# A hybrid decoder block: sums of input blocks taken from PSUM, and two plain projections made a pair of Strassen products

## The chip, the cores and the metric

The kernel runs on one core of a Trainium2 chip, in one launch. The metric is device time in microseconds, the median of several runs. Five engines work side by side and meet through semaphores: PE (TensorE, matrix products), DVE (VectorE), ACT (ScalarE), POOL (GpSimd) and SP (SyncE, which here only starts transfers). Each engine takes its own instructions in order.

## The reference

Sixteen learned tokens are put ahead of 1024 tokens of width 1024. One layer runs over the 1040 positions, and the output is the normalised rows of the 1024 real tokens.

```python
u = rms_norm(h, norm_w)
proj = u @ w_in                       # 1024 x 9232
(a_q, a_k, a_v, a_z, g_q, g_k, g_v, g_z, g_lr, gate_a, gate_b) = jnp.split(proj, ...)
...                                   # differential attention: a_q, a_k, a_v, a_z -> y_a
gk = (g_lr @ gla_gate_w2 + gla_gate_b).astype(jnp.float32)
lg = jax.nn.log_sigmoid(gk) / GLA_GATE_NORMALIZER
o_b = rms_norm(gla(qb, kb, vb, lg), gla_norm_w)   # gated linear attention
...                                   # y_b
merged = jax.nn.sigmoid(gate_a) * y_a + jax.nn.sigmoid(gate_b) * y_b
return h + merged @ w_out
```

The change concerns `u @ w_in` alone: how the columns g_q (four heads of 128) and g_k (four heads of 128) are made, and what is prepared for the other columns.

## The kernel before, in words

**Precision.** Every product is of float32 accuracy. Both operands are split into a high part in float32r (PE's one-pass format) and a low part, the rest; a product is three matmuls: high by high, high by low, low by high. ACT writes a high part (a copy), DVE or POOL the low part (a subtraction).

**Stage 1 (0 to about 111 us), lines 636 to 940.** Nine tiles of x (eight of 128 tokens and one of the 16 learned ones, the meta tokens) are loaded; ACT squares each with a running sum, DVE and POOL make the root, DVE scales the tile (`x_tile`). PE turns it around, chunk by chunk of 128 of the 1024 features, into PSUM (`u_chunk(g, kc)`: g is the half of the tokens, kc the chunk). ACT takes u_hi out of the bank, DVE u_lo. Beside it run the *plain* projections (`Jobs.cols`, lines 406 to 408): the four g_k tiles of 128 columns over all 1040 tokens in four pieces (`KP4`), and the g_q tiles 16 and 19 over the 1024 real tokens in two pieces of 512. Each piece is 24 matmuls into one of two banks, copied out by ACT (line 765, `stg`) and stored. The low-rank part of the gate (`lr_piece`) is of the same kind, with 48 columns and a chain of small steps on ACT and DVE behind it.

**The block sums, lines 829 to 863.** With u cut in halves by feature (i) and by token (j) into b_ij, Winograd's form of Strassen's product needs t1 = b12 - b11, t2 = b22 - t1, t3 = b12 - b22 and t4 = b21 - t2, split in two parts each. Before, each sum is made of the parts in SBUF, for each of four chunks k: three adds for t1 and t3 (high minus high, plus low, minus low), two for t2 and t4. t1, t2, t4 are DVE's, t3 is POOL's. A tile `bs` holds a sum till ACT has written its high part and DVE or POOL its low part.

**Stage 2, Strassen (from about 111 us).** `Strassen.run` takes two tiles of 128 columns at a time (a *pair*): seven products of half size, 12 matmuls of 512 columns each, 84 in all, where the plain way needs 96 (line 543). POOL makes the sums of weights (line 491), ACT and DVE split them (lines 225 and 226), DVE adds the results (line 557), ACT copies the first product out once in each pair (line 618). Before there are 21 such pairs, the g_q tiles 17 and 18 the first, and two of another form with the tokens on the partitions.

**Later stages.** Gated linear attention, differential attention, the two branch products and the output, from about 600 us on. The change does not touch them.

**What sets the order.** In stage 1 each operation is handed to `Schedule` with an engine, a rough duration, what it depends on, the ring of buffers that it takes and a priority; a simulation of the engines then writes the order of PE, DVE, ACT and POOL. So a new operation moves others on its engine. SP's order comes from the framework. Rings that matter: `X`, six PSUM banks for the turned chunks; `Y`, two banks for projections; `xt`, five tiles for x, and for the block sums later.

Of the kernel before, what the change touches and what calls it, by code (L numbers as in the profile page):

```python
# [10 lines left out]
F32 = mybir.dt.float32  # L11
# [35 lines left out]
GQ = False  # L47
NX = 5
XS = (0, 1, 2, 3, -1, 4, 5, 6, 7)
SCU = 0.6  # L50
T4E = "DVE"
# [18 lines left out]
class Schedule:  # L70
    """Puts operations in order: a simulation of the engines with rough durations, in which each takes
    the ready operation of the lowest priority number. A ring is a tile with so many buffers: an
    operation takes the next one, which is free when all operations that use it are done."""
# [18 lines left out]
    def run(self):  # L92
# [9 lines left out]
        def at(o):  # L102
            """when its data and its buffer are there"""
# [46 lines left out]
def tile_hybrid_block(  # L150
# [52 lines left out]
    for i in range(1, 5):  # L203
        tsum[i] = tuple(tpool.tile([P, KC // 2, 512], F32R, name=f"t{i}{p}") for p in "hl")
# [23 lines left out]
    # ---- weights and projections  # L228
# [15 lines left out]
    # what becomes of the projections  # L244
# [43 lines left out]
    def av_ev(g):  # L288
        """values of four heads, split, to DRAM"""
# [22 lines left out]
    def gv_ev(g):  # L312
        """values of two heads of the other branch, to DRAM"""
# [23 lines left out]
    class Jobs:  # L337
        """Projections as operations that fill the tensor engine; their sums go to the banks of ring Y."""
# [77 lines left out]
        def rows(self, src, evac, pre=None):  # L416
# [19 lines left out]
            # the first and last two in turns, for the weights of this job and of the next to come in time  # L436
# [15 lines left out]
    # ---- Winograd's form of Strassen's product: seven products of half the size for eight.  # L452
    # A: weights, halves by output column (two tiles of 128) and by row; B: halves by row and by token
    class Strassen:
# [72 lines left out]
        def run(self, over):  # L527
# [10 lines left out]
            def prod(ps, b, start):  # L538
                wh, wl = weights()
                bh, bl = self.b[b]  # L540
                for k in range(KC // 2):
                    for i, (w, x) in enumerate(((wh, bh), (wh, bl), (wl, bh))):
# [3 lines left out]
                            x[:, k],  # L546
# [13 lines left out]
            def prod_rows(ps, b, start, meta=()):  # L560
                # the first product in a bank clears it for both of its tiles of tokens
                bh, bl = self.b[b]
                for s in range(2):
                    wh, wl = weights()
                    for k, ti in ((2 * s + j, ti) for ti in range(4) for j in range(2)):
                        c, r = slice(P * ti, P * (ti + 1)), slice(256 * (ti % 2), 256 * (ti % 2 + 1))
                        for i, (x, w) in enumerate(((bh, wh), (bh, wl), (bl, wh))):
                            mm(  # L568
                                ps[ti // 2][:, r],
                                x[:, k, c],  # L570
# [62 lines left out]
    # ---- u^T = rms_norm([meta; x])^T, split into two float32r parts, and the first projections  # L633
# [3 lines left out]
    KP4 = ((0, 264), (264, 264), (528, 256), (784, 256))  # L637
    with ExitStack() as es:
# [49 lines left out]

        def u_chunk(g, kc):
# [13 lines left out]
            for p in range(2):  # L703
# [6 lines left out]
                    use=(own,), prio=10 * g + kc)  # L710
            U[g, kc] = lo

        def u_meta():
# [18 lines left out]
            def diff():  # L732
                """of the halves"""
# [24 lines left out]
        # g_q and g_k of the heads, by DRAM; the low-rank part of the gate  # L758
# [69 lines left out]
        # the sums of the blocks of u: t1 = b12 - b11, t2 = b22 - t1, t3 = b12 - b22, t4 = b21 - t2  # L828
        def sums(k):
            v = {}  # L830
            b = {
                (i, j): [t[:, k + 4 * i, NM + 512 * j : NM + 512 * j + 512].bitcast(F32) for t in (u_hi, u_lo)]
                for i in range(2)
                for j in range(2)
            }
            d = tuple(U[g, k + 4 * i] for g in range(2) for i in range(2))
            own = {}

            def term(name, eng, steps, deps, use):
                ring = "xt"  # L840
                f = tt if eng == "DVE" else nc.gpsimd.tensor_tensor
                us = 0.6 if eng == "DVE" else 1.2
                prev = d + deps

                for i, (x0, x1, o) in enumerate(steps):
                    def run(i=i, x0=x0, x1=x1, o=o):
                        if i == 0:
                            v[name] = s1.tile([P, 512], F32, name="bs", tag="xt", bufs=NX)
                        g = lambda y: v[y] if isinstance(y, str) else y
                        f(v[name], g(x0), g(x1), o)  # L850

                    prev = (op(eng, us, run, prev, take="" if i else ring, use=use, prio=30 + k),)
                    own[name] = own.get(name) or (ring, prev[0])
                hi, lo = (tsum[int(name[1])][p][:, k] for p in range(2))
                a = op("ACT", 0.48, lambda: nc.scalar.copy(hi, v[name]), prev, use=(own[name],), prio=30 + k)
                op(eng, us, lambda: f(lo, v[name], hi.bitcast(F32), ALU.subtract), (a,), use=(own[name],), prio=30 + k)
                return prev

            add, sub = ALU.add, ALU.subtract
            p1_ = term("t1", "DVE", [(b[0, 1][0], b[0, 0][0], sub), ("t1", b[0, 1][1], add), ("t1", b[0, 0][1], sub)], (), ())  # L860
# [1611 lines left out]
```

## Time and profile before

| what | value |
|---|---|
| median of 3 runs | 1407.32 us (1405.42 to 1411.9) |
| profiled execution, span from first to last instruction | 1406.7 us, 0.6 below the median (no other time of it is listed) |
| PE busy | 1339.3 us, 95% |
| DVE busy | 923.8 us, 66% |
| ACT busy | 734.2 us, 52% |
| POOL busy | 646.7 us, 46% |
| mean granted TensorE clock | 0.992 of full speed |
| chain that ended last | PE 66%, DVE 17%, issue 5%, DMA 5%, POOL 3%, ACT 3% |

A busy share is an average over stages with different limits, so a change in one stage has to be read from that stage. The chain of waits is followed back from the last instruction: at each step to what released it. Matmuls overlap in the records, so a matmul's cost is the distance between starts, or a window's time over its count, and not the duration of one.

### The profile page before, as it was taken

The numbers are of one execution on the slowest core, as the hardware profiler recorded it, in microseconds if no ns is written. First come the engines' busy times: TensorE is split into PE (matmuls) and PEld (weight loads), VectorE is DVE, ScalarE is ACT, GpSimd is POOL, SyncE is SP. The second block draws the span as 40 slices with busy tenths as digits, with TensorE's granted clock in tenths as the row PEclk, the third lists the DMA queues.
The fourth block names the chain that finished last, engine by engine and source line by source line (L and its number), as shares of the span: only waits on it lengthen the run. The fifth ranks groups of instructions, "written<-read, shape, count | busy, mean of one in ns | idle before, by whom it ended". The sixth has DMA issues, their size and how long they took to land.

```text
span 1406.7 us, 22441 instructions
## 1 busy us (share of the span) xinstructions
PE 1339.3 (95%) x7748; PEld 1159.6 (82%) x7748; DVE 923.8 (66%) x1613; ACT 734.2 (52%) x1596; POOL 646.7 (46%) x743
## 2 busy tenths in 40 slices
PE   7889999999999999988999989999999999999998
PEld 6877889889888888887888888888888888887786
DVE  5953563554656444469897887478777778647775
ACT  7333332563566656554545444468677776622343
POOL 3521332352355232226575565246676665535434
PEclk9999999999999999999999999999999999999999
DMA  6212674323422333285532456668865664578332
GB/s 219 86 57 90 195 254 137 105 105 109 141 98 105 112 113 113 97 272 160 184 103 98 139 185 204 212 204 287 300 190 183 207 218 144 204 274 284 136 116 87
DMA packets 126337, 229.50 MB, mean 163 GB/s; under 512 B 13568, under 2 KB 51648, under 8 KB 126224
## 3 DMA queue, kind: packets, MB, share of 16 engines
q1 hardware_dynamic: 125936, 227.03, 48.8%
q8 instruction: 61, 1.00, 0.3%
q0 software_dynamic: 288, 1.05, 0.3%
q14 instruction: 52, 0.43, 0.1%
HBM read 143.81 MB, written 84.21 MB: 162 GB/s over the span
## 4 chain that ended last, share of the span: by engine, by line
PE 66%; DVE 17%; issue 5%; DMA 5%; POOL 3%; ACT 3%; SPq 1%; POOLq 0%; DVEq 0%; ACTq 0%
PE ps_st L543 27%; PE ps_st L568 6%; DVE xl L1352 2%; PE ps_t L2268 2%; DVE bs L850 2%; PE ps_s L1645 2%; PE ps_s L1646 2%; PE ps_y L1928 2%; PE ps_proj L406 2%; PE ps_proj L407 1%; PE ps_proj L408 1%; PE ps_t L1759 1%; PE ps_l L1359 1%; PE ps_s L2268 1%; PE ps_y L2268 1%
## 5 line engine op out<-in xcount | busy, mean ns | idle before, releaser
L491 POOL TENSOR_TENSOR s<-w_raw 128x512 f32<-128x512 f32 x46 | 66.6, 1465 | 163.1 <-DMA w_raw<-in_w_col_dram 121.2
L1345 POOL TENSOR_TENSOR xl<-lg 128x128 f32<-128x128 f32 x224 | 108.3, 510 | 59.5 <-PE ps_l L1359 21.7
L406 PE MATMUL ps_proj<-u_hi,w_hi 128*128 128x346 f32 (+4 forms) x352 | 117.9, 335 | 8.8 <-ACT stg L765 5.2
L226 DVE TENSOR_TENSOR wl<-s,wh 128x512 fp32r<-128x512 f32 x92 | 73.2, 795 | 77.1 <-ACT wh L225 77.1
L407 PE MATMUL ps_proj<-u_lo,w_hi 128*128 128x346 f32 (+4 forms) x352 | 111.0, 315 | 0.0
L408 PE MATMUL ps_proj<-u_hi,w_lo 128*128 128x346 f32 (+4 forms) x352 | 110.9, 315 | 0.0
L225 ACT CAST wh<-s 128x512 fp32r<-128x512 f32 x92 | 56.8, 618 | 99.1 <-PE ps_st L543 52.6
L1674 DVE TENSOR_REDUCE nm<-ps_s 128x1 f32<-128x272 f32 (+7 forms) x128 | 96.5, 764 | 17.5 <-PE ps_s L1648 16.7
L1686 ACT ACTIVATE p<-ps_s,nm 128x272 f32<-128x272 f32 (+7 forms) x128 | 96.5, 755 | 19.4 <-DVE nm L1674 13.5
L543 PE MATMUL ps_st<-u_lo,wh 128*128 128x512 f32 x252 | 100.2, 398 | 0.0
L543 PE MATMUL ps_st<-u_hi,wh 128*128 128x512 f32 x252 | 99.4, 395 | 0.8 <-issue 0.8
L543 PE MATMUL ps_st<-u_hi,wl 128*128 128x512 f32 x252 | 99.1, 393 | 0.0
L225 ACT CAST wh<-w_raw 128x512 fp32r<-128x512 f32 x67 | 41.3, 617 | 91.1 <-PE ps_st L543 83.6
L226 DVE TENSOR_TENSOR wl<-w_raw,wh 128x512 fp32r<-128x512 f32 x67 | 58.6, 875 | 42.1 <-ACT wh L225 42.1
L491 POOL TENSOR_TENSOR s<-w_raw,s 128x512 f32<-128x512 f32 x21 | 27.1, 1292 | 120.2 <-DVE wl L226 120.2
L1698 POOL TENSOR_SCALAR p<-p,r,nlam 128x144 f32<-128x144 f32 (+3 forms) x64 | 56.4, 881 | 56.3 <-DVE r L1694 43.9
L406 PEld LDWEIGHTS ps_proj<-u_hi,w_hi 128*128 128x128 f32 x352 | 67.0, 190 | 12.7 <-ACT stg L765 6.0
L1645 PE MATMUL ps_s<-kk,q 128*128 128x264 f32 (+7 forms) x208 | 74.0, 360 | 2.1 <-ACT p L1686 1.9
L1703 DVE SCALAR_TENSOR_TENSOR p<-p,r,p 128x144 f32<-128x144 f32 (+3 forms) x64 | 67.8, 1060 | 11.1 <-POOL p L1698 10.9
L1646 PE MATMUL ps_s<-kk,q 128*128 128x264 f32 (+7 forms) x208 | 68.6, 334 | 0.0
L407 PEld LDWEIGHTS ps_proj<-u_lo,w_hi 128*128 128x128 f32 x352 | 66.9, 190 | 1.6
L408 PEld LDWEIGHTS ps_proj<-u_hi,w_lo 128*128 128x128 f32 x352 | 66.7, 190 | 1.4
(441 smaller groups left out, 4611.9 us busy)
## 6 DMA issues: line engine op xcount, KB each, us to landing
w_raw<-in_w_col_dram SPq DMA_DIRECT2D x54, 512.0 KB, 3.6
q<-d_q SPq DMA_DIRECT2D x32, 512.0 KB, 5.3
kk<-d_k SPq DMA_DIRECT2D x16, 520.0 KB, 6.1
d_g<-sg SPq DMA_DIRECT2D x32, 256.0 KB, 2.0
va<-d_v SPq DMA_DIRECT2D x16, 512.0 KB, 5.1
d_q<-qhi SPq DMA_DIRECT2D x24, 256.0 KB, 3.2
d_q<-qlo SPq DMA_DIRECT2D x24, 256.0 KB, 3.5
w_raw<-in_w_row_dram SPq DMA_DIRECT2D x12, 512.0 KB, 3.7
```

The lines of the kernel that those rows point to most:

```text
L225: nc.scalar.copy(hi, raw)
L226: (eng or nc.vector).tensor_tensor(lo, raw, hi.bitcast(F32), ALU.subtract)
L406: mm(b["ps"], wh, rh, start=kc == 0, stop=False)
L407: mm(b["ps"], wh, rl, start=False, stop=False)
L408: mm(b["ps"], wl, rh, start=False, stop=kc == KC - 1)
L491: nc.gpsimd.tensor_tensor(r, x, y, op)
L543: mm(ps, w[:, k], x[:, k], start=start and k == 0 and i == 0, stop=k == KC // 2 - 1 and i == 2, skip_group_check=not start,)
L1345: nc.gpsimd.tensor_tensor(dst, x if e else ref, ref if e else x, ALU.subtract)
L1645: mm(pp, qh, kk[:, c0 : c0 + w], start=True, stop=False)
L1646: mm(pp, ql, kk[:, c0 : c0 + w], start=False, stop=not has)
L1674: nc.vector.tensor_reduce(b, ps, AX.XY if len(ps.shape) == 3 else AX.X, ALU.max, negate=True)
L1686: act(dst, ps, AF.Exp, bias=b, accum_out=stat[t]["sm"][:, j : j + 1])
```

## The change

Three things are done together.

1. The block sums. When a chunk stands in its PSUM bank, ACT copies the exact chunk of the first token half to SBUF (line 743 of the new kernel, eight copies), and DVE subtracts from the bank of the second half (line 750, eight subtractions): that gives t1 and t2 without adding parts. t3 and t4 are one DVE subtraction each (line 891). The sums lie as whole float32 blocks in places that later hold other parts of t1 to t4 (`place`); only then are they split (lines 906 and 910). The setting `T4E` goes, and POOL takes no part.
2. `GQ = True`: the g_q tiles 16 and 19 are no plain projections any more, but a pair of Strassen's products, the third of stage 2. Two weights less are loaded and split in stage 1.
3. `KP4` is ordered anew: the g_k tiles begin with tokens 264 to 527, and the piece with the meta tokens comes second.

The diff, without the lines in which a comment or a blank line is all that differs:

```diff
-GQ = False
+GQ = True
-T4E = "DVE"
...
-        tsum[i] = tuple(tpool.tile([P, KC // 2, 512], F32R, name=f"t{i}{p}") for p in "hl")
+        tsum[i] = ([], [])
+    def tslot(i, e, k, dt=F32, name="tr"):
+        return tpool.tile([P, 512], dt, name=name, tag=f"t{i}{e}{k}")
...
-    KP4 = ((0, 264), (264, 264), (528, 256), (784, 256))
+    KP4 = ((264, 264), (0, 264), (528, 256), (784, 256))
...
+        def place(r):
+            n, i, k = r
+            if n == "b":
+                return k + 1, "hl"[i], 3
+            return (k + 1, "hl"[i], 2) if k < 2 else (3 + i, "h", 2)
...
+            i, k = divmod(kc, 4)
+            r = ("b", "t")[g], i, k
+            if g == 0:
+                def run():
+                    act(raw_tile(r), b["ps"], AF.Copy, scale=w)
+                R[r] = op("ACT", 0.55, run, prev, use=(own,), prio=12 + kc)
+            else:
+                x0 = ("t", 0, k) if i else ("b", 0, k)
+                def run():
+                    stt(raw_tile(r), b["ps"], w, raws[x0], ALU.mult, ALU.subtract)
+                R[r] = op("DVE", 0.67, run, prev + (R[x0],), use=(own,) + xuse(x0), take="xt" if r == ("t", 0, 3) else "",
+                          prio=10 * g + kc)
+                readers.setdefault(x0, []).append(R[r])
...
-            p1_ = term("t1", "DVE", [(b[0, 1][0], b[0, 0][0], sub), ("t1", b[0, 1][1], add), ("t1", b[0, 0][1], sub)], (), ())
-            p2_ = term("t2", "DVE", [(b[1, 1][0], "t1", sub), ("t2", b[1, 1][1], add)], p1_, (own["t1"],))
-            term("t3", "POOL", [(b[0, 1][0], b[1, 1][0], sub), ("t3", b[0, 1][1], add), ("t3", b[1, 1][1], sub)], (), ())
-            term("t4", T4E, [(b[1, 0][0], "t2", sub), ("t4", b[1, 0][1], add)], p2_, (own["t2"],))
+            for i in range(1, 5):
+                if i < 3:
+                    r = ("t", i - 1, k)
+                    ts[i], x[i] = R[r], r
+                    continue
+                r = ("b", i - 3, k)
+                def run(i=i, r=r):
...
+                    tt(dst, raws[r], raws["t", 1, k], ALU.subtract)
+                    raws[r] = dst
...
+                def hi(i=i):
+                    tsum[i][0].append(tslot(i, "h", k, F32R, "th"))
+                    nc.scalar.copy(tsum[i][0][k], raws[x[i]])
+                def lo(i=i):
+                    tsum[i][1].append(tslot(i, "l", k, F32R, "tl"))
+                    tt(tsum[i][1][k], raws[x[i]], tsum[i][0][k].bitcast(F32), ALU.subtract)
+                a = op("ACT", 0.48, hi, (ts[i],) + free("h") + last.get((i, 0), ()), prio=30 + k, use=use)
+                b = op("DVE", 0.6, lo, (a,) + free("l") + last.get((i, 1), ()), prio=30 + k, use=use)
```

The lines of the g_q pair stand in both kernels (`cols` without tiles 16 and 19 if `GQ`, and `stf.pairs.insert(2, ((w_col[16], w_col[19]), ...))`). After the last instruction of the second stage that differs, each engine's list is the same to its end.

Three places where the order moves. First ACT early in stage 1, from the last u_hi of the first token half to the squares of x tiles 4 to 7 (`sq`). Before:

```order
L708 ACTIVATE u_hi<-ps_x,nw 128x512 x6
L364 CAST w_hi<-w_raw 128x512 x2
L708 ACTIVATE u_hi<-ps_x,nw 128x512 x2
L364 CAST w_hi<-w_raw 128x512
L727 CAST um<-um_274 128x8x16
L668 ACTIVATE sq,ss<-xt 128x1024
```

Now, with `tr` the whole chunk of u:

```order
L368 CAST w_hi<-w_raw 128x512 x2
L743 ACTIVATE tr<-ps_x,nw 128x512 x3
L735 ACTIVATE u_hi<-ps_x,nw 128x512 x2
L368 CAST w_hi<-w_raw 128x512
L743 ACTIVATE tr<-ps_x,nw 128x512
L771 CAST um<-um_276 128x8x16
L743 ACTIVATE tr<-ps_x,nw 128x512 x2
L809 ACTIVATE stg<-ps_proj 128x264
L368 CAST w_hi<-w_raw 128x512
L783 CAST umd<-umd_296 128x4x16
L743 ACTIVATE tr<-ps_x,nw 128x512
L672 ACTIVATE sq,ss<-xt 128x1024
```

Seven of the eight copies stand ahead of the first of the four squares, the eighth ahead of the third. Second, DVE in the middle of stage 1, the block sums of the first two chunks and what stands between them (`bs` is a sum, `t2l` a low part of t2, `w_lo` that of a plain weight). Before:

```order
L850 TENSOR_TENSOR bs<-bs,u_lo 128x512
L850 TENSOR_TENSOR bs<-u_hi,bs 128x512
L850 TENSOR_TENSOR bs<-u_hi 128x512
L856 TENSOR_TENSOR t2l<-bs,t2h 128x512
L850 TENSOR_TENSOR bs<-bs,u_lo 128x512
L373 TENSOR_TENSOR w_lo<-w_raw,w_hi 128x512
L850 TENSOR_TENSOR bs<-bs,u_lo 128x512
L856 TENSOR_TENSOR t4l<-bs,t4h 128x512
```

Now (`th` and `tl` are the parts of any of the four sums), from the last of the subtractions in PSUM:

```order
L736 SCALAR_TENSOR_TENSOR u_lo<-ps_x,nw,u_hi 128x512
L750 SCALAR_TENSOR_TENSOR bs<-ps_x,nw,bs 128x512
L891 TENSOR_TENSOR tr<-tr 128x512 x2
L910 TENSOR_TENSOR tl<-tr,th 128x512 x4
L377 TENSOR_TENSOR w_lo<-w_raw,w_hi 128x512
L891 TENSOR_TENSOR tr<-tr 128x512 x2
```

The sums of a chunk are two adds and four low parts here. Third, PE at the step from stage 1 to Strassen (`ps_st`). Before, the end of g_q tile 19:

```order
L406 MATMUL ps_proj<-u_hi,w_hi 128x512
L407 MATMUL ps_proj<-u_lo,w_hi 128x512
L408 MATMUL ps_proj<-u_hi,w_lo 128x512
L543 MATMUL ps_st<-u_hi,wh 128x512
L543 MATMUL ps_st<-u_lo,wh 128x512
```

Now, the end of the low-rank part (`lrw`):

```order
L836 MATMUL ps_proj<-u_hi,lrw 48x256
L836 MATMUL ps_proj<-u_lo,lrw 48x256
L547 MATMUL ps_st<-u_hi,wh 128x512
L547 MATMUL ps_st<-u_lo,wh 128x512
L547 MATMUL ps_st<-u_hi,wl 128x512
```

The low-rank part stood ahead of g_k tile 3 and g_q tile 19 before; now it is the last work of stage 1, and g_k tile 3 stands right ahead of it.

## Rows read from the trace of the kernel before

**Rows 1.** Chain of waits, 0 to 130 us: share of each line.

```profile
by line: DVE bs L850 20.3%; PE ps_st L543 14.3%; PE ps_proj L406 9.1%; PE ps_proj L408 8.7%; PE ps_proj L407 8.7%; DMA subw<-in_subln_w_dram 4.6%; PE ps_x L700 4.3%; DVE t2l L856 3.6%; DVE w_lo L373 3.6%; DMA xt<-in_x_dram 3.4%; issue 3.2%;
```

**Rows 2.** Windows: stretch, its length, each engine's busy us and count, granted clock, DMA.

```profile
40.00:60.00 20.00, 18.40 (x137) 17.37 (x136) 19.84 (x22) 7.60 (x16) 10.90 (x7) 1.00 0.20 67
60.00:80.00 20.00, 13.82 (x99) 12.74 (x98) 19.76 (x23) 7.24 (x16) 8.44 (x6) 0.91 0.36 111
80.00:100.00 20.00, 17.65 (x142) 16.75 (x141) 10.28 (x18) 8.26 (x20) 5.28 (x4) 1.00 0.07 22
100.00:120.00 20.00, 19.22 (x84) 15.33 (x83) 1.98 (x3) 3.13 (x7) 1.28 (x1) 1.00 0.27 86
350.00:400.00 50.00, 50.00 (x234) 41.52 (x233) 29.51 (x38) 29.05 (x49) 20.16 (x15) 1.00 0.39 121
```

**Rows 3.** Chain of waits in order of time: start, us, what.

```profile
99.70 0.23 PE ps_proj L406
...
110.82 0.78 issue
111.60 18.59 PE ps_st L543 x80
```

**Rows 4.** Waits of PE, 0 to 130 us: us in total, times, longest.

```profile
PE ps_proj L406 <- ACT stg L765: 5.2, 3, 3.0
PE ps_proj L792 <- ACT stg L765: 2.6, 1, 2.6
PE ps_proj L792 <- DVE g L798: 1.3, 2, 0.8
PE ps_proj L406 <- DVE g L798: 1.0, 1, 1.0
```

**Rows 5.** Timeline of DVE, 40 to 81 us: start, duration, operation.

```profile
42.53 1.67 DVE L850 TENSOR_TENSOR bs<-u_hi,bs 128x512 f32<-128x512 f32 x1
...
54.44 0.68 DVE L850 TENSOR_TENSOR bs<-bs,u_lo 128x512 f32<-128x512 f32 x1
...
55.64 1.79 DVE L850 TENSOR_TENSOR bs<-u_hi,bs 128x512 f32<-128x512 f32 x1
...
80.06 1.79 DVE L850 TENSOR_TENSOR bs<-bs,u_lo 128x512 f32<-128x512 f32 x1
```

**Rows 6.** Timeline of POOL, 55 to 59 us.

```profile
55.18 1.70 POOL L856 TENSOR_TENSOR t3l<-bs,t3h 128x512 fp32r<-128x512 f32 x1 [8.13 <-DVE bs L850]
56.84 1.74 POOL L850 TENSOR_TENSOR bs<-u_hi 128x512 f32<-128x512 f32 x1
```

**Rows 7.** Timeline of ACT, two of the copies of a pair's first product.

```profile
114.95 0.58 ACT L618 COPY m<-ps_st 128x512 f32<-128x512 f32 x1
...
192.41 0.58 ACT L618 COPY m<-ps_st 128x512 f32<-128x512 f32 x1
```

**Rows 8.** Timeline of DVE, 28 to 90 us, other operations.

```profile
28.88 0.75 DVE L677 TENSOR_SCALAR xt<-xt,ss 128x1024 f32<-128x1024 f32 x1 [0.66 <-POOL ss L674]
...
32.31 4.70 DVE L709 SCALAR_TENSOR_TENSOR u_lo<-ps_x,nw,u_hi 128x512 fp32r<-128x512 f32 x7
...
37.58 1.31 DVE L880 CAST maskb<-maskf 128x256 bf16<-128x256 f32 x1
...
89.18 0.41 DVE L798 TENSOR_TENSOR g<-ps_proj,g 16x256 f32<-16x256 f32 x1
```

**Rows 9.** Timeline of ACT, 12 to 90 us.

```profile
13.10 3.58 ACT L708 ACTIVATE u_hi<-ps_x,nw 128x512 fp32r<-128x512 f32 x6 [0.48 <-PE ps_x L700]
...
26.89 1.05 ACT L668 ACTIVATE sq<-xt 128x1024 bf16<-128x1024 f32 x1
...
88.76 0.36 ACT L797 COPY g<-ps_proj 16x256 f32<-16x256 f32 x1
```

**Rows 10.** Windows of PE: length, busy us and matmuls, granted clock, DMA.

```profile
76.00:79.00 3.00, 2.98 (x14) 0.50 0.65 142
...
88.00:99.70 11.70, 11.70 (x97) 1.00 0.10 34
```

More of the change, by code (lines that the diff above doesn't have):

```diff
@@ L687, in tile_hybrid_block, with xuse, raw_tile @@
         xs = {i: x_tile(i) for i in XS}
+        R, raws, readers = {}, {}, {}
+        def xuse(r):
+            return (("xt", R["t", 0, 3]),) if r[0] == "t" and r[2] == 3 else ()
+        def place(r):
[3 more added lines that the diff above has]
+            return (k + 1, "hl"[i], 2) if k < 2 else (3 + i, "h", 2)
+        def raw_tile(r):
+            n, i, k = r
+            if n == "t" and k == 3:
+                if i == 0:
+                    raws["t3"] = s1.tile([P, 2, 512], F32, name="bs", tag="xt", bufs=NX)
+                raws[r] = raws["t3"][:, i]
+            else:
+                raws[r] = tslot(*place(r))
+            return raws[r]
         def u_chunk(g, kc):
@@ L710, in u_chunk @@
                     use=(own,), prio=10 * g + kc)
+            i, k = divmod(kc, 4)
[4 more added lines that the diff above has]
+                R[r] = op("ACT", 0.55, run, prev, use=(own,), prio=12 + kc)
+            else:
+                x0 = ("t", 0, k) if i else ("b", 0, k)
[4 more added lines that the diff above has]
+                readers.setdefault(x0, []).append(R[r])
             U[g, kc] = lo
@@ L826, in tile_hybrid_block @@
                     lr_piece(*p)
+        places = {place(r): r for r in R if r[0] == "b" or r[2] < 3}
         def sums(k):
[L830 to L857, printed above, removed]
@@ L859, in sums @@
-            add, sub = ALU.add, ALU.subtract
-            p1_ = term("t1", "DVE", [(b[0, 1][0], b[0, 0][0], sub), ("t1", b[0, 1][1], add), ("t1", b[0, 0][1], sub)], (), ())
-            p2_ = term("t2", "DVE", [(b[1, 1][0], "t1", sub), ("t2", b[1, 1][1], add)], p1_, (own["t1"],))
-            term("t3", "POOL", [(b[0, 1][0], b[1, 1][0], sub), ("t3", b[0, 1][1], add), ("t3", b[1, 1][1], sub)], (), ())
-            term("t4", T4E, [(b[1, 0][0], "t2", sub), ("t4", b[1, 0][1], add)], p2_, (own["t2"],))
+            ts, x = {}, {}
@@ new lines, in sums @@
+            for i in range(1, 5):
[5 more added lines that the diff above has]
+                def run(i=i, r=r):
+                    if k < 3:
+                        dst = raws[r]
+                    else:
+                        if i == 3:
+                            raws["b3"] = s1.tile([P, 2, 512], F32, name="bs", tag="xt", bufs=NX)
+                        dst = raws["b3"][:, i - 3]
+                    tt(dst, raws[r], raws["t", 1, k], ALU.subtract)
+                    raws[r] = dst
+                t = ts[i] = op("DVE", 0.6, run, (R[r], R["t", 1, k]) + tuple(readers.get(r, ())), prio=30 + k,
+                               take="xt" if k == 3 and i == 3 else "", use=xuse(("t", 1, k)) + ((("xt", ts[3]),) if k == 3 and i == 4 else ()))
+                readers.setdefault(("t", 1, k), []).append(t)
+                readers.setdefault(r, []).append(t)
+                x[i] = r
@@ new lines, in sums @@
+            for i in range(1, 5):
+                h, lo_ = tsum[i]
+                use = xuse(x[i]) + ((("xt", ts[3]),) if k == 3 and i > 2 else ())
+                free = lambda e: tuple(readers[places[i, e, k]]) if (i, e, k) in places else ()
+                def hi(i=i):
[6 more added lines that the diff above has]
+                b = op("DVE", 0.6, lo, (a,) + free("l") + last.get((i, 1), ()), prio=30 + k, use=use)
+                last[i, 0], last[i, 1] = (a,), (b,)
+                readers.setdefault(x[i], []).extend((a, b))
@@ L865, in tile_hybrid_block @@
+        last = {}
         for k in range(KC // 2):
@@ L900, in tile_hybrid_block @@
         op("DVE", 1.0, consts2, (c1,), prio=70)
-        uh = lambda k, t: tuple(v[:, 4 * k : 4 * k + 4, NM + 512 * t : NM + 512 * t + 512] for v in (u_hi, u_lo))
+        uh = lambda k, t: tuple([v[:, 4 * k + i, NM + 512 * t : NM + 512 * t + 512] for i in range(4)] for v in (u_hi, u_lo))
         blocks = {"b11": uh(0, 0), "b21": uh(1, 0), "b22": uh(1, 1)}
```

4 lines of the change are left out of this document (2 added, 2 removed).

## The prediction

> **What bounds the kernel now.** I read the chain of waits first, cut to the stretch from the start to 130 us. The reader is to see there that the largest share belongs to DVE on line 850, the adds that form the block sums of u, ahead of any line of PE [rows 1]. Next the windows: DVE is busy 19.8 of 20 us from 40 to 60 and again from 60 to 80, while PE has holes in the same stretch; from 100 on PE is nearly full and DVE idle, and a window in the Strassen stage is full on PE [rows 2]. So the first stage is bound by DVE until about 84 us, then by the projections that are left over, and Strassen's first product starts at 111.60 [rows 3]. Third, what PE waited for before that: the copy out of a bank on ACT (5.2 and 2.6 us) and the first add of the low-rank part on DVE (1.3 and 1.0), 10.1 us in all [rows 4]. ACT is in order, its copy stands behind the split of a block sum, and that waits for DVE; so these 10.1 us are DVE's delay as PE sees it.
>
> Fourth, why DVE is late: a 128x512 TENSOR_TENSOR takes 0.68 us in one row and 1.79 in the next, and the long ones lie where POOL runs one of its own [rows 5, 6]. There are 12 such long rows in a row of their own between 42.53 and 80.06, each about 1.1 over: 13 us of DVE time.
>
> **The change, part by part.** Everything after the Strassen stage keeps its order on all five engines, so the sum needs two numbers: when Strassen's first product starts, and how much longer the Strassen stage is.
>
> *Two plain g_q tiles go.* One is the last projection before Strassen: 48 matmuls from 99.70 to 110.82, 11.1 us, 0.232 each [rows 3]. The other has the same 48, at the start of each half of the stage. Removed from PE: 22.2 us.
>
> *One Strassen pair comes.* Each pair copies its first product once; four pairs lie between the copies at 114.95 and 192.41 [rows 7], so one costs 77.46/4 = 19.4 us. PE is full there, so all of it is on the path. By itself the exchange is worth 2.8 us.
>
> *The block sums.* Before, DVE did 40 operations for them (28 adds, 12 low parts) and POOL 16. Now DVE does 8 subtractions straight from PSUM, 8 adds, 16 low parts: 32; POOL none; ACT 8 more copies from PSUM. Two plain weights less are four low parts less on DVE. POOL's share in this stage shrinks to the weights before 23 us and three sums of the first Strassen weights, so the 13 us of stretching go. What is new is the cost of a subtraction with one input in PSUM and one in SBUF; the nearest row is u_lo of the same shape, 7 in 4.70 us, 0.67 each [rows 8]. Ends: 0.60 (as back-to-back adds in SBUF) and 1.79 (a stretched add); I take 0.67.
>
> Here a rule speaks against the change. The Trainium skill, "Perfetto Trace Analysis", section Optimizing Scalar/DVE Operations, says that a saturated DVE may be relieved by giving work to other engines, GpSimd among them, and warns that the two share a port; the change takes POOL's help away. By the relief alone DVE would get about 8 x 0.60 = 4.8 us more; by [rows 5, 6] the help cost DVE more than it took. The rows decide.
>
> *ACT's eight copies, early.* Their price: six evictions of this shape from PSUM take 3.58 us, 0.6 each [rows 9], so 4.8 us. They stand between and before the squares of x tiles 4 to 7 (the ACT rows in the section on the change), where ACT had little idle time. The last square was at 26.89 and the last tile was scaled from 28.88 to 29.63 [rows 8, 9]. Bounds of the delay: 1.5 us (ACT's holes swallow most) and 6 (the copies, plus a later load of the last x tile, which now stands behind a store in SP's queue). I take 4: tile 7 is ready at 33.6.
>
> *From there to Strassen.*
> 1. Transposes and the first u_hi, 0.7 us: DVE starts its pass at 34.3. It has 16 operations from PSUM in place of 8: 16 x 0.67 = 10.7, so the last u_lo is there at 45.0.
> 2. PE goes through the first of the six second-half pieces as the chunks come, and is done with it at 45.3. Work before that isn't the limit: the first halves of three g_k tiles are 144 matmuls of 0.1225 us, 17.6 us, as much as g_q's half and g_k's pieces were before.
> 3. Five pieces more: 120 matmuls of 256 columns. Tile g_k 3, of 264 and 256 columns, ran undisturbed from 88 to 99.7: 97 matmuls in 11.70 us [rows 10], 0.1206 each, so 0.1225 and 0.119 by width; 120 x 0.119 = 14.2: 59.5.
> 4. Tile g_k 3: 96 x 0.1206 = 11.6, so 71.1.
> 5. The low-rank part now comes last: 64 matmuls of such widths at 0.12: 7.7, so 78.8.
> 6. Strassen's first bank waits for the last low-rank sum: a copy on ACT (0.36) and an add on DVE (from 89.18, 0.41) [rows 8, 9] with the handovers 1.0: 79.8.
> 7. Left over of the waits of [rows 4]: 0 at the low end, 7.8 (ACT's two) at the high end. DVE has from 45.0 only 8 adds, 16 low parts, 2 low parts of a weight at 0.60 and the constants, some 2.6 us with 1.31 for the longest [rows 8], 18 us in all: done near 63, or 67 with its waits on ACT. A copy that is up to 2.4 us late costs PE nothing, since a second bank is being filled for 2.8. I take 0.7: **start at 80.5**.
>
> The first Strassen weights are no limit: three POOL sums at about 1.3 us after DVE's end, a cast and a low part, ready near 71. If DVE ended 10 us later they would be. The three POOL sums can stretch at most three DVE operations by 1.1 each, at a time when DVE has slack.
>
> *Sum.* 80.5 - 111.6 = -31.1; +19.4; net -11.7. The profiled execution's span is 1406.7 us, so the changed kernel's is 1395.0; the median of the runs, 1407.3, stands 0.6 above the span: **1395.6 us**. A check from the other side: 22.2 us of work, 10.1 of waits and 1.5 of slow clock (3 us of matmuls at half the clock from 76 to 79 [rows 10]) could go, 33.8 in all; the sum uses 31.1 of it.
>
> **The rivals.**
>
> *PE's waits stay (1402.7 us).* If ACT's splits still wait on DVE in turns, and the copies out of the banks behind them, the 7.8 us of ACT's waits in [rows 4] stay, instead of the 0.7 counted: start at 87.6, 1402.7. For it: 16 splits in an in-order queue, as before. Against: DVE's queue is 17 us shorter than PE's.
>
> *The stretching isn't POOL's (1401 us).* If long adds come from something else, DVE's 24 operations after 45.0 would again average about 1.1 us [rows 5], 27 us and the constants: 75; the weights 7 us after that, 82, and PE's waits with them, 86 at most: 1401. Against it: the long rows match POOL's in time, and the short ones its pauses.
>
> *The clock falls (slower, 1414.4 to 1421.9 us).* The place is the plain projections after 45 us. PE now idles in two stretches before that, waiting for the late x tiles and for DVE's longer pass. Before, after waits of this kind, PE was granted 0.50 of full speed, which is the 1.2 GHz level, from 76 to 79, and 1.00, 2.4 GHz, after [rows 10]. A matmul of this width costs 0.119 us at the upper level and 2.98/14 = 0.213 at the lower [rows 10], 0.094 more. It decides from 11.7/0.094 = 124 of the 280 matmuls after 45 us; with 200 of them low the time is 1414.4, with all 1421.9. Against: the one fall in the rows lasted 3 us. The Trainium skill, "TensorE: Matmul & The Clock Gate", section HAM oscillation, has such a case: a kernel whose gaps between groups of matmuls sent the clock down in each round; the trace here shows one fall only.
>
> *The change doesn't do what it says.* The pair might cost more than 19.4 us if POOL's sums or weights came late in the Strassen stage; in the late window PE is busy 50.00 of 50 us [rows 2], so there is no slack to hide it in, but nothing that points to it; I give it no price of its own: each us of it is a us of the time, and it takes 11.7 to undo the gain.
>
> **How the numbers follow.** Chances: forecast 0.68; waits stay 0.13; not POOL 0.07; clock 0.04; the rest, unnamed, 0.08, on both sides. The likeliest's own range: step 7 from 0 to 3.5 and the x delay from 1.5 to 6 give 1392.4 to 1400.4, and 1.5 for how runs scatter (1405.4 to 1411.9 before) goes on the low side: 1391 to 1400. To take in the lower part of the second and third case the range goes from 1390 to 1402. About 0.5% (7 us: below 1400.3 or above 1414.4) is what a measurement can tell from no change. Faster: the forecast, 0.05 of waits that stay in part, 0.05 of the rest: 0.78. Same: 0.08 of the waits, and the third case: 0.15. Slower: the clock and 0.03 of the rest: 0.07.
>
> **What would show it.** Right: no POOL work between 24 us and the first Strassen sums; no DVE operation of 512 over 0.8 us there; u's pass on DVE ends at 43 to 47; Strassen's first product at 78 to 84; an added pair of 19.4 us; everything after earlier by 11 to 12 us. Wrong: DVE adds of 1.7 us with POOL idle, PE waits on ACT's copies above 4 us, a granted clock of 0.5 after 45 us, or a start after 88. The forecast is wrong altogether if the stage starts Strassen in time and the end does not come earlier by as much: then something behind the Strassen stage takes the time back.

## The result, and the profile after

The changed kernel takes 1396.45 us (median of 7 runs, 1393.72 to 1400.65), the kernel before, run beside it, 1405.44 (7 runs, 1402.94 to 1411.9): 0.9925 of the time, with an interval of 0.9907 to 0.9944. Forecast were 1395.6 us, in a range of 1390 to 1402. The profiled execution of the changed kernel is its slowest, 1400.65 us with a span of 1398.9.

The chain of waits of the changed kernel from 0 to 130 us, the share of each line:

```profile
by line: PE ps_st L547 38.7%; PE ps_proj L412 9.2%; PE ps_proj L411 9.2%; PE ps_proj L410 9.2%; DMA xt<-in_x_dram 7.6%; PE ps_proj L836 5.8%; DMA subw<-in_subln_w_dram 4.8%; ACT u_hi L735 3.3%; PE ps_x L727 3.2%; issue 1.8%; ACT w_hi L368 1
```

DVE's block sums, which led this list before [rows 1], are not among its first lines any more. What is left of the first stage in the chain is the projections on PE, the low-rank part among them (L836), and the load of x. The windows of the changed kernel, with the columns of [rows 2]:

```profile
20.00:40.00 20.00, 18.50 (x150) 17.39 (x149) 13.67 (x30) 16.88 (x35) 3.58 (x6) 1.00 0.61 210
40.00:60.00 20.00, 20.00 (x171) 20.00 (x170) 18.59 (x31) 11.39 (x24) 0.00 (x0) 1.00 0.34 100
60.00:80.00 20.00, 19.00 (x160) 18.75 (x159) 9.25 (x24) 8.05 (x21) 3.76 (x3) 1.00 0.19 60
```

From 40 to 80 DVE was busy 39.6 us before and is 27.8 now; PE was busy 32.2 and is 39.0. POOL has nothing from 40 to 60. The waits of PE from 0 to 130 us (us in total, times, longest) answer to [rows 4]:

```profile
PE ps_x L727 <- DVE ss L675: 8.6, 2, 7.2
PE ps_x L727 <- DVE xt L681: 1.3, 2, 1.0
PE ps_st L547 <- issue: 1.0, 1, 1.0
PE ps_proj L410 <- DVE u_hi L773: 0.8, 1, 0.8
PE ps_x L727 <- ACT tr L743: 0.6, 1, 0.6
...
```

The four rows of before, 10.1 us, are gone: PE waits neither for a copy out of a projection's bank nor for a low-rank sum. The largest row, 8.6 us for the norm of the first x tiles, stood before too, with 8.3, and is the start of the program. The end of the stage, from the same chain cut to 76 to 130 us (start, us, what), answers to [rows 3]:

```profile
75.95 2.91 PE ps_proj L836 x25
78.86 1.00 issue
79.86 50.32 PE ps_st L547 x218
```

Strassen's first product starts at 79.86 us in place of 111.60, against 80.5 forecast. DVE in the changed kernel, from the last x tile to the last low part of a sum (start, us, operation), answers to [rows 5, 8]:

```profile
32.50 0.75 DVE L681 TENSOR_SCALAR xt<-xt,ss 128x1024 f32<-128x1024 f32 x1 [0.66 <-POOL ss L678]
...
34.40 1.41 DVE L750 SCALAR_TENSOR_TENSOR tr<-ps_x,nw,tr 128x512 f32<-128x512 f32 x2 [0.94 <-ACT u_hi L735]
35.72 2.06 DVE L736 SCALAR_TENSOR_TENSOR u_lo<-ps_x,nw,u_hi 128x512 fp32r<-128x512 f32 x3
...
44.28 0.74 DVE L750 SCALAR_TENSOR_TENSOR bs<-ps_x,nw,bs 128x512 f32<-128x512 f32 x1
...
61.64 0.28 DVE L933 CAST maskb<-maskf 128x256 bf16<-128x256 f32 x1
...
63.37 0.69 DVE L910 TENSOR_TENSOR tl<-bs,th 128x512 fp32r<-128x512 f32 x1 [0.17 <-ACT th L906]
```

A subtraction with one input in PSUM (L750) takes what u_lo takes (L736), and no single operation of 512 columns is longer than 0.74 there. The timeline of POOL in the changed kernel has one gap between the last row of the x tiles and the first Strassen sums, where [rows 6] had its block sums:

```profile
31.91 0.55 POOL L678 TENSOR_TENSOR ss<-ss,mhalf 128x1 f32<-128x1 f32 x1 [0.93 <-DVE ss L675]
64.28 2.52 POOL L495 TENSOR_TENSOR s<-w_raw 128x512 f32<-128x512 f32 x2 [31.82 <-DVE tl L910]
```

The timeline of ACT in the changed kernel: three of the copies of u, and the first and the last of six copies of a pair's first product, as in [rows 7]:

```profile
17.90 1.89 ACT L743 ACTIVATE tr<-ps_x,nw 128x512 f32<-128x512 f32 x3
...
83.35 0.59 ACT L622 COPY m<-ps_st 128x512 f32<-128x512 f32 x1
...
180.11 0.58 ACT L622 COPY m<-ps_st 128x512 f32<-128x512 f32 x1
```

Five pairs lie between the last two rows, 96.76/5 = 19.35 us each. The net at the Strassen stage is therefore 79.86 - 111.60 + 19.35 = -12.4 us, and the copy that stood at 192.41 in [rows 7] has its like in the one at 180.11, 12.3 earlier. The spans of the two profiles differ by 1406.7 - 1398.9 = 7.8 only. Where the other 4.6 went is read from windows of PE in the later stages (length, busy us and matmuls, granted clock, DMA). The changed kernel:

```profile
808.00:812.00 4.00, 3.59 (x18) 0.57 0.20 52
...
910.00:925.00 15.00, 12.50 (x65) 0.77 0.30 96
```

From 100 us on the clock is granted in full but for a few short stretches, of which two stand here. At 808 to 812 it is 0.57 on the mean, so a part of that ran at the 1.2 GHz level; 4 x 0.43 = 1.7 us are lost there. Not all of them are at the same places in each run, and experiments 4 and 5 below count them. By the prediction's own sign (Strassen in time, the end not earlier by as much) this profile alone would speak against it.

### The profile page after: what moved, and what is told of

Its sections match the earlier page's. It is cut to its first block, busy times and chain, and to the rows that moved or that the text cites. A ratio compares the mean times of both kernels' runs of the same rounds, so it can differ in the third digit from the quotient of the medians.

```text
span 1398.9 us, 22432 instructions
## 1 busy us (share of the span) xinstructions
PE 1337.4 (96%) x7736; PEld 1158.8 (83%) x7736; DVE 908.3 (65%) x1613; ACT 741.1 (53%) x1608; POOL 626.1 (45%) x731
## 4 chain that ended last, share of the span: by engine, by line
PE 67%; DVE 13%; DMA 5%; issue 5%; POOL 5%; ACT 4%; SPq 1%; POOLq 0%; DVEq 0%; ACTq 0%
PE ps_st L547 28%; PE ps_st L572 6%; DVE xl L1405 3%; PE ps_t L2321 2%; PE ps_s L1698 2%; PE ps_proj L410 2%; PE ps_proj L412 2%; PE ps_proj L411 2%; PE ps_l L1412 2%; PE ps_s L1699 1%; PE ps_y L2321 1%; PE ps_s L2321 1%; PE ps_t L1812 1%; PE ps_y L1981 1%; PE ps_y L1983 1%
## 5 line engine op out<-in xcount | busy, mean ns | idle before, releaser
L547 PE MATMUL ps_st<-th,wh 128*128 128x512 f32 x352 | 137.3, 390 | 0.2 <-DVE u L561 0.2
L547 PE MATMUL ps_st<-tl,wh 128*128 128x512 f32 x352 | 137.1, 389 | 0.0
L547 PE MATMUL ps_st<-th,wl 128*128 128x512 f32 x352 | 136.9, 389 | 0.0
L410 PE MATMUL ps_proj<-u_hi,w_hi 128*128 128x346 f32 (+3 forms) x320 | 105.1, 329 | 3.2 <-DVE cc L561 1.7
L547 PE MATMUL ps_st<-u_hi,wh 128*128 128x512 f32 x264 | 104.2, 395 | 1.0 <-issue 1.0
L411 PE MATMUL ps_proj<-u_lo,w_hi 128*128 128x346 f32 (+3 forms) x320 | 99.0, 309 | 0.1
L412 PE MATMUL ps_proj<-u_hi,w_lo 128*128 128x346 f32 (+3 forms) x320 | 98.3, 307 | 0.0
L230 DVE TENSOR_TENSOR wl<-w_raw,wh 128x512 fp32r<-128x512 f32 x70 | 59.8, 854 | 49.7 <-ACT wh L229 49.7
L547 PEld LDWEIGHTS ps_st<-th,wh 128*128 128x128 f32 x352 | 66.1, 188 | 14.8 <-ACT sg L273 0.6
L547 PEld LDWEIGHTS ps_st<-th,wl 128*128 128x128 f32 x352 | 66.1, 188 | 14.0
L547 PEld LDWEIGHTS ps_st<-tl,wh 128*128 128x128 f32 x352 | 66.1, 188 | 13.8
```

What stands on the lines that cost most here:

```text
L230: (eng or nc.vector).tensor_tensor(lo, raw, hi.bitcast(F32), ALU.subtract)
L410: mm(b["ps"], wh, rh, start=kc == 0, stop=False)
L411: mm(b["ps"], wh, rl, start=False, stop=False)
L412: mm(b["ps"], wl, rh, start=False, stop=kc == KC - 1)
L547: mm(ps, w[:, k], x[k], start=start and k == 0 and i == 0, stop=k == KC // 2 - 1 and i == 2, skip_group_check=not start,)
```

## The experiments

Experiments 1 to 4 share 22 runs of the kernel before (median 1404.61), 6 to 8 share 14 (median 1406.04). My theory: DVE's queue bound the first stage, for two causes, its own adds and POOL's beside them, and with both gone PE's own work sets the start of Strassen. Rivals: the help of POOL was worth its price; the eight copies on ACT or the new order of the pieces carries a part; the gain comes from the pair.

**1. The kernel before, with t3's sums on DVE in place of POOL.**

```diff
-            term("t3", "POOL", [(b[0, 1][0], b[1, 1][0], sub), ...
+            term("t3", "DVE", [(b[0, 1][0], b[1, 1][0], sub), ...
```

> The kernel before, with t3 made by DVE and not by POOL: 16 operations more on DVE, none of the block sums on POOL. Theory (POOL's adds stretch DVE's): 56 operations at 0.60 us, 33.6, in place of 40 at 0.60 and 13 us of stretching, 37; the low-rank part then follows about 3 us sooner, Strassen's first product starts near 108 (111.6 before), the time falls by about 3 us, and no 512-wide DVE add takes over 0.8 us. Rival (the long adds come from something else): 16 operations more at the old mean of 0.9 to 1.0 us, so Strassen starts at 120 to 127 and the time rises by 9 to 15 us.

Measured: 1399.16 us (9 runs), ratio 0.9962 [0.9946, 0.9979]; Strassen's first product at 105.79. DVE's timeline in this kernel, where [rows 5] had its long adds:

```profile
42.74 0.69 DVE L850 TENSOR_TENSOR bs<-u_hi,bs 128x512 f32<-128x512 f32 x1
...
82.38 0.69 DVE L856 TENSOR_TENSOR t4l<-bs,t4h 128x512 fp32r<-128x512 f32 x1
```

With POOL idle no add is stretched, and the last low part is there at 83.1, where it ended at 84.4 with POOL's help: DVE does all the work of both and is done earlier. The Trainium skill, "Perfetto Trace Analysis", section Optimizing Scalar/DVE Operations, allows for giving work of a full DVE to GpSimd, with the warning that the two share a read port; here the warning is the part that decides. The waits of PE in this kernel, 0 to 120 us:

```profile
...
PE ps_proj L406 <- DVE g L798: 5.7, 1, 5.7
...
PE ps_proj L792 <- DVE g L798: 0.4, 2, 0.2
```

The 10.1 us of [rows 4] are 6.1 here, nearly all in one piece: the low-rank sum stands in DVE's queue behind the block sums. Those 4.0 us less are most of the 5.8 that the start moved; the other 1.8 I can't assign to a row. The clock doesn't account for them: its fall in this stage cost 3.4 us here (0.51 on the mean from 77 to 84) and about 1.7 before (the one at 76 to 79 [rows 10]). The expectation of 3 was too low.

**2. The kernel before, with the pair alone.**

```diff
-GQ = False
+GQ = True
```

> The kernel before with the two g_q tiles as a Strassen pair and nothing else changed. Theory (DVE bounds stage 1): DVE has only 4 low parts less, so it is done with the sums near 82 and the low-rank part and Strassen's first weights follow; first product at 88 to 92, plus 19.4 for the pair: the time falls by 0 to 4 us, of which the exchange of 22.2 for 19.4 is 2.8. Rival (PE's projections were the bound, and the pair alone brings the gain): first product near 80, the time falls by 10 to 12 us.

Measured: 1407.55 us (12 runs), ratio 1.0017 [1.0003, 1.0032]; first product at 91.51, as the theory had it. Of the 22.2 us taken off PE the start moves by 20.1, and the pair takes 19.4: 0.7 is left at the Strassen stage, and by the medians the kernel is a little slower, where 0 to 4 us less were expected. PE's waits in this kernel, 0 to 120 us, and its busy time up to the first product, before and here:

```profile
...
PE ps_proj L406 <- ACT stg L765: 5.3, 3, 4.2
PE ps_proj L406 <- DVE u_lo L730: 3.4, 1, 3.4
...
```

```profile
sum 111.60, PE 91.40; mean PE 22.85
...
sum 91.51, PE 71.49; mean PE 17.87
```

PE is idle for 20.2 us before and 20.0 here, so the work taken off does not come back as more waiting in sum. The waits change their place: 3.4 us are new and stand early, where the plain g_q half was and where PE now waits for the meta tokens (L730) that the first of g_k's pieces takes. What is missing is busy time: it falls by 19.9 and not by 22.2, since more matmuls run slowly. The clock was 0.57 on the mean from 65 to 73, 3.4 us lost for about 1.7 before, and after the early wait 15 matmuls of 264 columns start 0.22 us apart, from 21.41 to 24.85, and 0.12 later. The runs also had a lower mean clock than those of the kernel before beside them, 0.990 for 0.993, which is about 4 us and more than the difference of the medians. So it is not shown that DVE is what keeps the pair from paying. The early wait is the one that the new order of the pieces removes in experiment 8; a run with the pair and that order, but with the old sums, was not made.

**3. The change without the pair.**

```diff
-GQ = True
+GQ = False
```

> The changed kernel with the two g_q tiles left as plain projections: new block sums and new order of g_k's pieces alone. Theory (with DVE relieved, PE's work is what is left): first product 22.2 us later than in the changed kernel, near 102 (111.6 before), no added pair: the time falls by about 9.6 us in all, so that this and the pair's 2.8 make up the 12.3 by which Strassen's copies came earlier. Rival (the sums only turn DVE's delay into other waits): first product at 107 or later, the time falls by under 4 us.

Measured: 1394.67 us (6 runs), ratio 0.9919 [0.9895, 0.9944]; first product at 100.42, 11.2 us earlier than before with no pair to pay for. By the medians that is 9.9 us, against 9.6 expected. The sums with the new piece order are nearly all of the gain: PE is idle for 11.5 us up to the first product, where it was 20.2 before. Set against the whole change, the pair adds 100.42 - 79.86 - 19.35 = 1.2 us at the Strassen stage, and the ratios of this kernel and of experiment 4 can't be told apart. The windows of PE in this kernel and then in the changed one show why it is not the 2.8 of the forecast:

```profile
13.00:20.00 7.00, 7.00 (x30) 1.00 0.11 21
20.00:30.00 10.00, 9.92 (x75) 1.00 0.84 302
...
sum 100.40, PE 88.89; mean PE 17.78
```

```profile
13.00:20.00 7.00, 6.39 (x34) 1.00 0.07 20
20.00:30.00 10.00, 8.95 (x71) 1.00 0.92 326
...
sum 79.80, PE 67.12; mean PE 13.42
```

PE's busy time falls by 21.8 us, but its idle time up to the first product grows from 11.5 to 12.7: the plain g_q half had filled PE while x tiles were still on their way. What the subtractions from PSUM bring by themselves was not run. If the parts add, the 5.8 of experiment 1 and the 3.6 to 4.2 of experiment 8 leave some 1 to 2 of the 11.2 us for them and ACT's copies, an estimate from these three starts; t3's engine and the order of the pieces would then be most of the gain.

**4 and 5. The changed kernel and the kernel before, once more, unedited.**

> The changed kernel once more. In its first profile Strassen came 12.4 us earlier than before and the end only 7.8 earlier; the difference arose at 800 to 870 and at 1235 to 1320 us, where PE was granted half its clock in two stretches (808 to 812, 1286 to 1290) that the kernel before did not have in its profile. Theory (where the clock falls late is chance): Strassen's first product again at 79.9 within 0.3, other stretches at half the clock, and a span that is lower by about 1.7 us for each such stretch less. Rival (the change gives time back behind Strassen): the same loss at the same two places, the end again 7 to 8 us earlier than the profile of before.

> The kernel before once more, for a second trace. Theory (late falls of the clock are chance): Strassen's first product again at 111.6 within 0.5, the falls behind 600 us at partly other places, and the span differs from 1406.7 by about 1.7 us for each stretch more or less. Rival: the same stretches at the same places, span within 0.5 of 1406.7.

Measured: the changed kernel 1393.02 us (4 runs), ratio 0.9907 [0.9881, 0.9933], span 1392.0, first product at 80.42, 0.6 later than in the first profile where 0.3 were allowed; the kernel before 1407.65 in its one run, span 1405.9, first product at 111.96. Windows of PE of the changed kernel's second profile, the same two stretches:

```profile
808.00:812.00 4.00, 3.32 (x27) 1.00 0.20 52
...
910.00:925.00 15.00, 14.76 (x110) 1.00 0.67 218
```

The same program, and the falls at 808 and in 910 to 925 are not there. Others come again: from 635 to 643 the clock is 0.79 on the mean in both profiles, and near 1310 both have a fall (0.60 from 1316 to 1320 in the first, 0.67 from 1308 to 1312 here). Length times what is missing to a full clock, summed over windows of 4 us from 100 us to the end, gives 13.7 us in the first profile of the changed kernel and 7.2 in this one: 6.5 apart, and the spans are 6.9 apart. The two profiles of the kernel before have 10.2 and 10.0. At the loss of the kernel before, the first profile of the changed kernel would have gained 7.8 + 13.7 - 10.2 = 11.3 us. So of the 4.6 us that went, the falls account for 3.5, and they come and go in one and the same program; 1.1 us behind Strassen's start stay unassigned.

**6. The changed kernel, with t3's subtraction and low part on POOL.**

```diff
-                    tt(dst, raws[r], raws["t", 1, k], ALU.subtract)
+                    (nc.gpsimd.tensor_tensor if i == 3 else tt)(dst, raws[r], raws["t", 1, k], ALU.subtract)
...
-                    tt(tsum[i][1][k], raws[x[i]], tsum[i][0][k].bitcast(F32), ALU.subtract)
+                    f = nc.gpsimd.tensor_tensor if i == 3 else tt
+                    f(tsum[i][1][k], raws[x[i]], tsum[i][0][k].bitcast(F32), ALU.subtract)
...
```

> The changed kernel with t3's subtraction and low part given back to POOL (4 of each). Theory (DVE has some 15 us of slack now): DVE adds beside POOL's take 1.7 us again, up to 8 of them, but Strassen's first product stays within 0.7 us of 79.9 and the time the same. Rival (the sums still bound the stage): first product 4 us later or more, or earlier by what DVE no longer does.

Measured: 1395.98 us (4 runs), ratio 0.9927 [0.9904, 0.995]; first product at 81.72, 1.3 to 1.9 later than in the two profiles of the changed kernel, where the theory allowed 0.7 and the rival wanted 4. DVE, then POOL, of this kernel:

```profile
41.38 0.74 DVE L750 SCALAR_TENSOR_TENSOR tr<-ps_x,nw,tr 128x512 f32<-128x512 f32 x1
...
45.86 5.18 DVE L911 TENSOR_TENSOR tl<-tr,th 128x512 fp32r<-128x512 f32 x3
50.97 0.68 DVE L891 TENSOR_TENSOR tr<-tr 128x512 f32<-128x512 f32 x1
...
58.19 0.68 DVE L911 TENSOR_TENSOR tl<-bs,th 128x512 fp32r<-128x512 f32 x1
...
58.85 1.32 DVE L934 CAST maskb<-maskf 128x256 bf16<-128x256 f32 x1
```

```profile
40.89 2.62 POOL L891 TENSOR_TENSOR tr<-tr 128x512 f32<-128x512 f32 x2 [8.69 <-DVE tr L750]
...
47.05 1.74 POOL L911 TENSOR_TENSOR tl<-tr,th 128x512 fp32r<-128x512 f32 x1
...
56.71 3.31 POOL L911 TENSOR_TENSOR tl<-tr,th 128x512 fp32r<-128x512 f32 x1 [6.21 <-ACT th L906]
```

Three low parts on DVE take 5.18 us, 1.73 each, while POOL runs its rows of 1.74; the next one, with POOL idle, 0.68. POOL pays too: 1.31 each for two rows while DVE reads PSUM, and 1.74 beside DVE's adds in SBUF. Which of the two pays can change: the POOL row at 56.71 takes 3.31 while DVE's low parts beside it stay at 0.68, and then a cast on DVE with one input in SBUF takes 1.32, which takes 0.28 in the changed kernel with POOL idle. DVE's operations from PSUM keep their 0.74 beside POOL. PE now waits 1.6 us for a copy out of a bank. The stretch is brought back at will, at a small price, since DVE is no bound any more.

**7. The changed kernel without ACT's eight copies.**

```diff
-                def run():
-                    act(raw_tile(r), b["ps"], AF.Copy, scale=w)
-                R[r] = op("ACT", 0.55, run, prev, use=(own,), prio=12 + kc)
+                raws[r] = dst[0].bitcast(F32)
+                R[r] = hi
...
-                    tt(dst, raws[r], raws["t", 1, k], ALU.subtract)
+                    tt(dst, u_hi[:, 4 * (i - 3) + k, NM : NM + 512].bitcast(F32), raws["t", 1, k], ALU.subtract)
```

> The changed kernel without ACT's eight early copies: the block sums take u_hi of the first token half in place of the whole block, so the low part of that half is left out of them. Theory of the prediction (late x tiles put off DVE's pass, and that the projections): x tile 7 scaled 3.5 to 4 us sooner, near 29.6; DVE's pass ends near 41; first product 4 us sooner, 76. Rival (PE is full from 13 us on, so that its work alone sets the start): the tile sooner as well, but the first product only by PE's holes between 13 and 40, some 2 to 3 us: near 77.5.

Measured: 1395.73 us (5 runs), ratio 0.9933 [0.9906, 0.9959]; first product at 78.83, 1.0 to 1.6 earlier. DVE in this kernel, the last x tile and the start of its pass:

```profile
28.62 0.75 DVE L681 TENSOR_SCALAR xt<-xt,ss 128x1024 f32<-128x1024 f32 x1 [0.67 <-POOL ss L678]
...
30.52 1.41 DVE L748 SCALAR_TENSOR_TENSOR tr<-ps_x,nw,u_hi 128x512 f32<-128x512 f32 x2 [0.34 <-ACT u_hi L735]
```

Both stand 3.9 us earlier than with the copies, and only about a third of it reaches Strassen: less than the rival's 2 to 3 us, and far from the theory's 4.

**8. The changed kernel with the piece order of before.**

```diff
-    KP4 = ((264, 264), (0, 264), (528, 256), (784, 256))
+    KP4 = ((0, 264), (264, 264), (528, 256), (784, 256))
```

> The changed kernel with g_k's pieces in the old order, the one with the meta tokens first. Theory: PE then waits for the meta tokens' chunk at its first piece, at 15 to 21 us, in place of later work: first product 0 to 3 us later (79.9 to 83), time up by as much. Rival: no change at all, since the first pieces only fill time before the x tiles come: within 0.3 us.

Measured: 1399.31 us (10 runs), ratio 0.9956 [0.9936, 0.9976]; first product at 84.05, 3.6 to 4.2 later, above the 0 to 3 expected. The timeline of PE in this kernel (start, us, operation, and in brackets the idle time before it and what ended it):

```profile
18.88 1.97 PE L727 MATMUL ps_x<-ident,xt 128*128 128x128 f32 x8 [3.15 <-ACT tr L743]
20.79 1.03 PE L766 MATMUL ps_x<-ident,xt 16*128 16x16 f32 x8
23.77 0.59 PE L410 MATMUL ps_proj<-u_hi,w_hi 128*128 128x264 f32 x1 [1.95 <-DVE u_hi L773]
24.15 0.42 PE L411 MATMUL ps_proj<-u_lo,w_hi 128*128 128x264 f32 x1
24.37 0.42 PE L412 MATMUL ps_proj<-u_hi,w_lo 128*128 128x264 f32 x1
```

The first piece with the meta tokens needs their transposes (L766) and u_hi of them (L773), and these stand behind transposes that wait for ACT's copies: 3.2 + 1.9 us of waiting. In the changed kernel the piece from token 264 on runs in that time, and the two waits are 0.6 and 0.8. After the waits the matmuls start 0.22 us apart until 26.57, and 0.12 from there on, though the column of the granted clock reads 1.00: 12 of them, about 1.2 us, where the changed kernel has such a stretch only up to 16.5. Up to the first product PE is idle for 16.1 us here and for 12.7 in the changed kernel's first profile, so most of the delay is waiting and the rest this pace.

## Why the prediction was right, step by step

**The start of the pass** was right in sum. The copies cost 0.63 us each (1.89 for three in a row), 0.6 were counted; tile 7 was ready at 33.25 against 33.6, DVE began at 34.40 against 34.3 and ended at 44.94 against 45.0, at 0.66 us per operation where 0.67 was taken from [rows 8]. The 4 us of delay were chosen between two bounds, and the rows show another way to them than ACT's time: the first of the squares waits for its tile, whose load is issued 2.3 us later than before and takes longer. SP's rows before and in the changed kernel, then ACT's first of the four squares there:

```profile
17.57 1.76 SPq L660 DMA_DIRECT2D xt<-in_x_dram  x4
```

```profile
19.86 1.28 SPq L664 DMA_DIRECT2D xt<-in_x_dram  x3
...
24.29 0.37 SPq L664 DMA_DIRECT2D xt<-in_x_dram  x1
```

```profile
25.45 1.06 ACT L672 ACTIVATE sq<-xt 128x1024 bf16<-128x1024 f32 x1 [0.37 <-DMA xt<-in_x_dram]
```

Before, that square stood at 21.21. Without the copies, in experiment 7, the four loads are issued from 17.80 again. That the x buffers come free later because PE's turning of the chunks waits for banks that ACT still copies (the 0.6 us of PE behind `tr`, L743) fits, but was not tried apart; a weight's load ahead of them in SP's queue, at 18.89, may have a part.

**PE from there on** was right to a few tenths. The low-rank part's first product was to start at 71.1 and did so at 71.11; its end was put at 78.8 and came at 78.86. The six second-half pieces ended at about 59.8 against 59.5. The pieces ran at the full clock here: the windows of the changed kernel show 12.00 us busy of 12 with 103 matmuls from 59 to 71, granted 1.00.

**The last handover**: 1.00 us from the last product to Strassen's first, as in step 6. **Step 7**, what is left of PE's waits, was put at 0.7 and is about nothing. That is the 0.6 between 80.5 and 79.86.

**POOL's stretching** was the right reading of [rows 5, 6], and experiments 1 and 6 show it from both sides. But its size on the path was understated where it was tried alone, 5.8 us for the 3 expected: what it delays on DVE is waited for on PE by way of the low-rank sum, which shows 4.0 of them.

**The exchange of two g_q tiles for a pair** was wrong as a term of its own. Its parts were right (22.2 off, 19.4 on; measured 21.8 and 19.35), but "worth 2.8 by itself" was too much. Alone it brought 0.7 at the Strassen stage and nothing in time (ratio 1.0017), with the new sums 1.2 at the Strassen stage: the plain g_q half had covered waits early in the stage, and without it PE is idle 1.2 us longer, or, in the old piece order, waits 3.4 us for the meta tokens.

**The late x tiles** were a term of the sum, 4 us, carried one to one from tile 7 to Strassen. Experiment 7 takes 3.9 away and gains 1.0 to 1.6: PE has other work in that time, and steps 2 to 5 counted it as work behind the pass. **The piece order** was costed at nothing and is worth 3.6 to 4.2 us in the first product, because it covers what the copies delay. Taken by the runs, the first stage's limit is the work that PE can do from 13 us on, not the moment of the last x tile; the chain counted in steps 1 to 6 ends at the same time since PE has little idle time left on either path: 3.1 us in the changed kernel from 13 us to the first product.

**The rivals.** PE's waits that stay: gone, by the rows of PE's waits. Stretching that isn't POOL's: ruled out by experiments 1 and 6. The clock that falls: PE was granted 1.00 in each window from 20 to 100 us, with 20.00 us busy of 20 from 40 to 60; the stretches of late x tiles, 1.5 us of idle time from 20 to 40, brought no fall. Experiments 1 and 2, where PE waits longer in one piece in the plain projections (5.7 and 4.2 us), did have one: 0.51 over the 7 us from 77 to 84, and 0.57 over the 8 from 65 to 73, 3.4 us lost in each; so did both profiles of the kernel before. So the place was rightly named, and in the changed kernel PE had no such wait there. That the trace of before shows one fall only holds for its first stage; behind 600 us it has four more stretches (at 648, 832, 924 and 1324 us).

**From -12.4 to the medians.** The first set of runs gives 9.0 us, the second 11.6. The Strassen start is 0.6 us apart in the two profiles, and the other difference that the traces show is the late falls of the clock. The runs without a trace say the same: each has a mean granted clock, and the span times what is missing to 1, taken off the time, leaves 1385.3 to 1388.2 us for the seven runs that lie between 1393.72 and 1400.65. What makes some falls come in one run and not in another of the same program stays open.

That the median lies within 0.9 us of 1395.6 is in part luck. The gain forecast was 11.7 us and the gain of that set is 9.0; but the forecast set out from a median of three runs of the kernel before, 1407.32, and the median of its seven is 1405.44, from which the same 11.7 would have given 1393.7. The profiled execution of before took longer than the median as well: the time of the changed kernel's is 1.75 us above its span, so a span of 1406.7 belongs to some 1408.4 us and not to the median.

## What to carry to other kernels

Before a helper engine is given adds of the engine that is full, look whether the helped engine's rows get longer in just those stretches; here the same adds took 0.69 us alone and 1.73 beside POOL. Work taken off an engine may have covered a wait, so the idle time of that engine up to the stage's end is to be compared before and after, and not the work alone; the pair was worth 0.7 to 1.2 us here for 2.8 counted. A delay at the head of a chain counts only by what the waiting engine can't fill: count its idle time up to the stage's end, not the latest arrival.

## What the runs showed of the hardware

A subtraction on DVE with one input in PSUM and one in SBUF, 128x512, costs what the split of a chunk costs, 0.66 us, 16 of them in turn from 34.40 to 44.94. DVE and POOL hold each other up where both take their inputs from SBUF. In turns, DVE's adds go from 0.69 to 1.73 us and POOL's from 1.31 to 1.74; at another place a POOL row takes 3.31 while DVE's adds beside it stay at 0.68. It does not need two inputs on DVE: a 128x256 cast with one input in SBUF takes 1.31 and 1.32 us beside POOL ([rows 8], experiment 6) and 0.28 with POOL idle. DVE's operations with an input in PSUM kept their 0.74 us beside POOL's rows of 1.31.

After a wait early in the first stage PE's matmuls of 264 columns start 0.22 us apart and later 0.12, while the column of the granted clock reads 1.00 (experiment 8, 23.77 to 26.57 us): there the distance of the starts has to be read, not the column. Falls of the granted clock in one and the same program differ in number and in part of their places from run to run: 13.7 us were lost to them behind 100 us in one profile of the changed kernel, and 7.2 in the next, with those near 640 and near 1310 us in both.
